# Expert, modulation and compression weights in slabs of 8 KB per partition, and two groups of thin products regrouped

## The chip, the cores and the metric
One core of a Trainium2 chip runs the whole program. The time is device microseconds of one execution from launch to end; lower is better. Times of the kernel before: 2248.72, 2251.83 and 2254.51 us, median 2251.83 us.

## What is computed
Three transformer blocks in a row on one sequence of 256 tokens with width 1024, all in float32, batch 1.

- Block 1: a normalized projection, two attention mixers (block attention with 8 heads, and an attention with compressed, selected and windowed keys, 8 heads), gates, an output projection. The compressed keys and values come from 15 windows of 32 tokens in two groups: `gelu(win @ w1) @ w2`, with w1 of 2048 x 256, once for keys and once for values.
- Block 2: two layers. Each is modulated by six vectors of 1024, `silu(c) @ ada_w + ada_b` with ada_w of 1024 x 6144 per layer (in the first layer, two of them for a second vector too). Layer 0 mixes by attention and a 31-tap convolution, layer 1 by a short convolution. Both end in 16 experts: each expert takes its 32 best tokens and computes `(silu(x @ gate) * (x @ up)) @ down`, three matrices of 1024 x 1024, that is 4 MB each. The experts of the two layers are 402 MB of weights, more than half of all that is read.
- Block 3: two layers with differential attention and gated linear attention, cross attention to a memory, and a feed-forward network with a 3-tap convolution.

## The kernel before
All loads of weights go through SyncE's queue (SP) in slabs of up to 1 MB, 128 partitions by 2048 floats. Buffers for them are the ring (`slab`, L320): four in block 1, seven in block 2.

*Dense weights* (`weights`, L383) come from one array that the host packs so that each slab is contiguous, 8 KB per partition. Each is split in pieces of 128 x 1024 into a high half `wh` (ACT, L376) and a rest `wl` (VectorE, L377), in two tiles with three buffers each. A dense product is three matmuls (L408 to L410): high by high, rest by high, high by rest. In `rows` the halves are the moving operand, in `columns` the stationary one. After each slab, `step` lets a generator (`fill`) put in some of the modulation's work.

*Modulation* (`Ada.steps`, L960): 12 chunks of 512 columns per layer, each in two slabs that take four rows of 2 KB per partition straight from the matrix (L975). In 6 of the 24 chunks VectorE multiplies and adds, in the other 18 PE does: the vector is the stationary operand with 32 columns, of which one or two are filled, and each of four row tiles has a column group of its own (L979), with 512 columns of output. The four groups are summed after an ACT copy (L1000), four transposes (L1002) and a VectorE sum (L1004).

*Compression* (`compress`, L724): windows `wn` are made from transposed keys and values (L738, L746). Each w1 comes in two slabs with eight rows of 1 KB per partition (L751). 16 products per matrix of 256 columns (L755) add up in one column group for keys and one for values. An element-wise chain (L758 to L766), two transposes (L769) and w2 (L775) follow. On POOL's queue the bias table of the attention is written to memory and read back meanwhile (`toeplitz`, L667 and L670); attention reads it first in `nsa(0)` (L605).

*Experts* (`moe`, L1320): a quarter of a matrix is a slab. `place` (L1338) puts slab after slab into a rotation of 21 places: seven buffers of the ring, seven of `more`, three pairs of split buffers (two DMAs of 512 KB), and four tiles that are free in this stage, one of them (`xv`) made of four quarters of 256 KB. A place is loaded again once PE has used it. The row tiles k and k + 1 stand in a partition as two rows of 4 KB. A slab is eight products of 256 columns on four column groups (L1359). Expert 15's down weights are taken by columns instead (`down`, L1487), in rows of 1 KB, so that output columns finish one after the other; then come the next layer's first steps.

The convolution of layer 0 (`gated`, L1115) writes its input to memory (L1128) and reads it back in four shifted copies (L1132), on SP's queue too.

The order of instructions on each engine is made by the compiler's scheduler from the program order, priorities and modelled durations; SP issues in that order and stops at each DMA whose buffer isn't free.

Of the kernel before, what the change touches and what calls it, by code (L numbers as in the profile page):

```python
# [87 lines left out]

def _pack_dense(inp):
    flat = np.empty(DENSE_SIZE, np.float32)  # L90
# [178 lines left out]
class Kern:  # L269
# [113 lines left out]
    def weights(self, key, g, chunks=None, gain=None):  # L383


        for at, k0, nk, width in (OFF[key][g] if chunks is None else [OFF[key][g][c] for c in chunks]):
# [286 lines left out]
def block1(k, ada):  # L673
# [4 lines left out]
    with ExitStack() as cx:  # L678
# [45 lines left out]
        def compress():  # L724
# [33 lines left out]
            h = ea.tile([64, 256], F32, name="cmp_x")  # L758
            nc.scalar.copy(h, hid[:64, :256])
            z = ea.tile([64, 256], F32, name="cmp_z")  # L760
# [7 lines left out]
            for f in range(2):  # L768
                nc.tensor.transpose(p[:, 64 * f:64 * f + 64], z[:, 128 * f:128 * f + 128], k.ident[:64, :64])  # L769
            ht = ea.tile([128, 2, 64], F32, name="cmp_ht")  # L770
            nc.scalar.activation(ht, p[:, :128].rearrange("p (f s) -> p f s", f=2), AF.Copy, scale=0.5)
# [171 lines left out]
class Ada:  # L943
# [16 lines left out]
    def steps(self, l, which, chunks=range(12)):  # L960
# [4 lines left out]
        for c in chunks:  # L965
# [7 lines left out]
            for h in range(2):  # L973
                w = k.slab(2048).rearrange("p (k f) -> p k f", f=512)
                nc.sync.dma_start(w, k.a["ada_w_2"][l, 512 * h:512 * h + 512, 512 * c:512 * c + 512].rearrange("(k p) f -> p k f", p=128))  # L975
                for kt in range(4):
                    if not vec:
                        with k.tc.issue_after(self.behind.ins) if self.behind is not None else ExitStack():
                            nc.tensor.matmul(acc[32 * kt:32 * kt + 32], self.st[:, 4 * h + kt], w[:, kt], start=h == 0, stop=h == 1,  # L979
                                             tile_position=(0, 32 * kt))  # L980
# [7 lines left out]
                if h == 1:  # L988
# [9 lines left out]
                    else:  # L998
                        ms = k.sm.tile([128, 512], F32, tag="sq", name="ada_ms", bufs=1)
                        nc.scalar.copy(ms, acc)  # L1000
# [1003 lines left out]
```

## Time and profile before

| | |
|---|---|
| profiled execution | 2254.34 us, span 2252.5 us |
| granted clock, mean | 0.888 |
| PE busy | 1853.4 us (82%), 14677 matmul instructions |
| VectorE busy | 1026.7 us (46%) |
| ACT busy | 723.6 us (32%) |
| DMA | 638.00 MB, mean 283 GB/s |
| block 1 | 0 to about 320 us |
| layer 0 up to the routing, experts | to about 540, to 994 us |
| short convolution, routing, experts | to about 1125, to 1577 us |
| block 3 | to the end |

PE's busy time counts pipelined matmuls, so a busy PE is not PE at its peak. A float32 product counts as two matmul instructions (x16 is eight products), a split one as one. The DMA share is the busy time of the 16 DMA engines and can pass 1, since a packet's record overlaps the next. A chain of waits is the work that ended last, followed back from the end: start, duration, engine or transfer, tile and line. A transfer in it lasts from issue to landing and so includes the time that it stands behind others.

### The profile page before, as it was taken

The page shows a single profiled execution, that of the slowest core. Times are in us where ns is not written, and L with a number is a line of the kernel's source. Part 1 is how long each engine was busy: PE and PEld are TensorE (multiplying, and loading weights), DVE is VectorE, ACT ScalarE, POOL GpSimd, SP SyncE. Part 2 cuts the span into 40 slices and gives each one's busy share as a digit, 9 for nine tenths or more (in the row PEclk, how much of TensorE's full clock was granted, in tenths as well). Part 3 has the DMA queues.
Part 4 walks back from the last instruction along what each step waited for, and adds up shares of the span by engine and source line. Part 5 has one row for each costly group of instructions (what it writes and reads, how often), then busy time and mean ns, then how long its engine had stood idle before and what let it go on. Part 6 is the DMA issues. An engine that isn't in the chain of part 4 may idle for free.

```text
span 2252.5 us, 35590 instructions
## 1 busy us (share of the span) xinstructions
PE 1853.4 (82%) x14677; PEld 1275.5 (57%) x14677; DVE 1026.7 (46%) x2282; ACT 723.6 (32%) x1360; POOL 53.0 (2%) x94
## 2 busy tenths in 40 slices
PE   7999998888766666679886666666998999999999
PEld 5777875455322222249642222222776998888997
DVE  5785675444100000048510000002876996678984
ACT  3444444342000000025300000001665665555663
POOL 1000010101000000000100000000100000000000
PEclk9999999998887777789897777777999999999999
DMA  9664588867999999997799999999632455344453
GB/s 256 238 211 167 204 299 285 295 227 259 408 408 408 408 408 405 408 396 303 258 404 408 408 408 408 406 408 393 199 133 79 165 187 178 123 138 160 171 178 121
DMA packets 176466, 638.00 MB, mean 283 GB/s; under 512 B 12158, under 2 KB 27390, under 8 KB 157872
## 3 DMA queue, kind: packets, MB, share of 16 engines
q1 hardware_dynamic: 173504, 627.03, 73.9%
q0 software_dynamic: 1360, 4.49, 1.1%
q10 hardware_dynamic: 1440, 4.21, 0.5%
q8 instruction: 115, 1.88, 0.3%
q14 instruction: 47, 0.39, 0.0%
HBM read 632.96 MB, written 2.72 MB: 282 GB/s over the span
## 4 chain that ended last, share of the span: by engine, by line
PE 51%; DMA 37%; DVE 6%; ACT 3%; issue 2%; SPq 0%; POOL 0%; ACTq 0%; DVEq 0%
DMA w<-in_moe_w_up 6%; DMA more<-in_moe_w_gate 4%; DMA wl<-in_moe_w_up 4%; PE up L410 4%; PE up L409 4%; PE up L408 4%; DMA more<-in_moe_w_up 3%; PE gu L1359 3%; DMA w<-in_moe_w_down 3%; DMA more<-in_moe_w_down 2%; PE down L408 2%; PE down L410 2%; PE down L409 2%; DMA wl<-in_moe_w_down 2%; DVE wl L377 2%
## 5 line engine op out<-in xcount | busy, mean ns | idle before, releaser
L377 DVE TENSOR_TENSOR wl<-w,wh 128x1024 fp32r<-128x1024 f32 (+5 forms) x316 | 377.3, 1198 | 172.5 <-ACT wh L376 165.7
L376 ACT CAST wh<-w 128x1024 fp32r<-128x1024 f32 (+5 forms) x316 | 320.7, 1021 | 285.4 <-PE down L409 63.4
L1458 ACT ACTIVATE hd<-gu 128x256 f32<-128x256 f32 x32 | 12.3, 384 | 746.5 <-PE gu L1359 746.5
L1459 DVE SCALAR_TENSOR_TENSOR hd<-hd,gu 128x256 f32<-128x256 f32 x32 | 13.5, 421 | 500.0 <-ACT hd L1458 500.0
L1359 PE MATMUL gu<-w,xst 128*32 128x256 f32 x1376 | 125.3, 496 | 74.2 <-DMA w<-in_moe_w_up 43.1
L409 PE MATMUL up<-ff_xh,wl 128*128 128x256 f32 x608 | 171.0, 283 | 2.7 <-DVE wl L377 2.7
L410 PE MATMUL up<-ff_xl,wh 128*128 128x256 f32 x608 | 170.1, 283 | 1.2 <-DVE ff_xl L377 1.2
L408 PE MATMUL up<-ff_xh,wh 128*128 128x256 f32 x608 | 168.5, 284 | 2.4 <-ACT ff_xh L376 2.4
L1359 PE MATMUL gu<-more,xst 128*32 128x256 f32 x1344 | 112.1, 466 | 56.3 <-DMA more<-in_moe_w_up 30.3
L1359 PEld LDWEIGHTS gu<-w,xst 128*32 128x32 f32 x1376 | 44.6, 132 | 150.2 <-DMA w<-in_moe_w_up 70.6
L409 PEld LDWEIGHTS up<-ff_xh,wl 128*128 128x128 f32 x608 | 116.2, 191 | 3.1 <-DVE wl L377 3.1
L1473 DVE SCALAR_TENSOR_TENSOR ysm<-dn,gcol,moe_mq 128x256 f32<-128x256 f32 x30 | 14.5, 484 | 226.7 <-PE dn L1359 226.7
L410 PEld LDWEIGHTS up<-ff_xl,wh 128*128 128x128 f32 x608 | 115.2, 190 | 1.5 <-DVE ff_xl L377 1.5
L408 PEld LDWEIGHTS up<-ff_xh,wh 128*128 128x128 f32 x608 | 114.4, 191 | 2.8 <-ACT ff_xh L376 2.8
L1359 PEld LDWEIGHTS gu<-more,xst 128*32 128x32 f32 x1344 | 44.7, 127 | 119.0 <-DMA more<-in_moe_w_up 53.4
L408 PE MATMUL down<-wh,ff_h 128*128 128x512 f32 x176 | 69.7, 396 | 0.0
L409 PE MATMUL down<-wh,ff_l 128*128 128x512 f32 x176 | 69.6, 396 | 0.0
L1359 PE MATMUL dn<-more,ht 128*32 128x256 f32 x672 | 56.3, 483 | 14.1 <-DMA more<-in_moe_w_down 9.6
L1359 PE MATMUL dn<-w,ht 128*32 128x256 f32 x672 | 56.9, 480 | 9.3 <-ACT ht L1465 5.2
L410 PE MATMUL down<-wl,ff_h 128*128 128x512 f32 x176 | 63.7, 395 | 0.0
L409 PE MATMUL w_in_b<-xh,wl 128*128 128x256 f32 x192 | 56.4, 295 | 2.8 <-DVE wl L377 2.8
L408 PE MATMUL w_in_b<-xh,wh 128*128 128x256 f32 x192 | 55.2, 296 | 2.0 <-ACT wh L376 2.0
(643 smaller groups left out, 4031.9 us busy)
## 6 DMA issues: line engine op xcount, KB each, us to landing
w<-in_wd SPq DMA_DIRECT2D x144, 1024.0 KB, 5.0
w<-in_ada_w SPq DMA_DIRECT2D x48, 1024.0 KB, 6.5
w<-in_moe_w_gate SPq DMA_DIRECT2D x48, 1024.0 KB, 14.6
more<-in_moe_w_up SPq DMA_DIRECT2D x48, 1024.0 KB, 18.5
w<-in_moe_w_down SPq DMA_DIRECT2D x46, 1024.0 KB, 18.0
more<-in_moe_w_down SPq DMA_DIRECT2D x46, 1024.0 KB, 18.6
w<-in_moe_w_up SPq DMA_DIRECT2D x38, 1024.0 KB, 15.6
more<-in_moe_w_gate SPq DMA_DIRECT2D x36, 1024.0 KB, 18.5
```

The lines of the kernel that those rows point to most:

```text
L376: self.nc.scalar.copy(hi, src)
L377: self.nc.vector.tensor_tensor(lo, src, hi.bitcast(F32), op=OP.subtract)
L408: mm(out, lh, rh, start=first, stop=False)
L409: mm(out, ll, rh, start=False, stop=False)
L410: mm(out, lh, rl, start=False, stop=last)
L1359: nc.tensor.matmul(out[32 * c:32 * c + 32], lhs(kt), w(1024 * kk + 256 * c, 256), start=kt == 0, stop=kt == 7, tile_position=(0, 32 * c))
L1458: nc.scalar.activation(hd, gu[:, 0:256], AF.Tanh, scale=0.5)
L1459: nc.vector.scalar_tensor_tensor(hd, hd, 1.0, gu[:, 0:256], op0=OP.add, op1=OP.mult)
L1473: nc.vector.scalar_tensor_tensor(y, dn[:, :256], gcol[:, e:e + 1], mq, op0=OP.mult, op1=OP.mult)
```

## The change
The host lays out the expert, modulation and first compression matrices anew, so that every slab is one contiguous megabyte with 8 KB per partition; expert 15's down weights in the order of its column quarters. The DMAs that load them take whole rows of 8 KB (only the place made of four quarters keeps four DMAs, with rows of 2 KB). To have an 8 KB place there too, `wh` and `wl` become the two halves of one tile `ws` with three buffers, for dense weights as for experts.

The compression product is split: each of keys and values is computed in two halves of 128 columns in two column groups, which makes four groups with 128 columns each. The chain behind it works on 128 x 128 instead of 64 x 256, with one transpose.

The modulation product keeps four column groups and uses them otherwise: row tiles kt and kt + 2 share one, and the 512 columns are split in two halves of 256. That makes 16 products of 256 columns per chunk instead of eight of 512, a copy of 256 columns, two transposes instead of four, and a sum over two groups, one sum per vector.

```diff
+def _lay_out(inp):
+    for n in ("moe_w_gate_2", "moe_w_up_2", "moe_w_down_2"):
+        w = inp[n]
+        s = w.reshape(2, 16, 4, 2, 128, 1024).transpose(0, 1, 2, 4, 3, 5).reshape(2, 16, 4, 128, 2048)
+        if n == "moe_w_down_2":
+            s = s.copy()
+            s[:, 15] = w[:, 15].reshape(2, 8, 128, 4, 256).transpose(0, 3, 2, 1, 4).reshape(2, 4, 128, 2048)
+        inp[n] = s
+    inp["ada_w_2"] = inp["ada_w_2"].reshape(2, 2, 4, 128, 12, 512).transpose(0, 4, 1, 3, 2, 5).reshape(2, 12, 2, 128, 2048)
+    for n in ("cmp_w1_k", "cmp_w1_v"):
+        inp[n] = inp[n].reshape(1, 2, 8, 128, 256).transpose(0, 1, 3, 2, 4).reshape(1, 2, 128, 2048)
...
-                wh, wl = (self.sp.tile([128, 1024], F32R, tag=z, name=z)[:, :m * width].rearrange("p (k c) -> p k c", c=width)
-                          for z in ("wh", "wl"))
+                ws = self.sp.tile([128, 2048], F32R, tag="ws", name="ws")
+                wh, wl = (ws[:, z:z + m * width].rearrange("p (k c) -> p k c", c=width) for z in (0, 1024))
...
-                    nc.sync.dma_start(w.rearrange("p (l f) -> p l f", f=256),
-                                      a[nm][1024 * half:1024 * half + 1024].rearrange("(l p) f -> p l f", p=128))
+                    nc.sync.dma_start(w, a[nm][half])
                     for l in range(8):
                         lp = 8 * half + l
-                        nc.tensor.matmul(hid[32 * i:32 * i + 32, :256], wn[:, i, lp].rearrange("p g c -> p (g c)"),
-                                         w[:, 256 * l:256 * l + 256], start=lp == 0, stop=lp == 15,
-                                         tile_position=(0, 32 * i))
+                        for f in range(2):
+                            b = 32 * (2 * i + f)
+                            nc.tensor.matmul(hid[b:b + 32, :128], wn[:, i, lp].rearrange("p g c -> p (g c)"),
+                                             w[:, 256 * l + 128 * f:256 * l + 128 * f + 128], start=lp == 0, stop=lp == 15,
+                                             tile_position=(0, b))
...
-                nc.sync.dma_start(w, k.a["ada_w_2"][l, 512 * h:512 * h + 512, 512 * c:512 * c + 512].rearrange("(k p) f -> p k f", p=128))
+                nc.sync.dma_start(w.rearrange("p k f -> p (k f)"), k.a["ada_w_2"][l, c, h])
...
-                            nc.tensor.matmul(acc[32 * kt:32 * kt + 32], self.st[:, 4 * h + kt], w[:, kt], start=h == 0, stop=h == 1,
-                                             tile_position=(0, 32 * kt))
+                            for z in range(2):
+                                q0 = 32 * (2 * (kt % 2) + z)
+                                nc.tensor.matmul(acc[q0:q0 + 32, :256], self.st[:, 4 * h + kt], w[:, kt, 256 * z:256 * z + 256],
+                                                 start=h == 0 and kt < 2, stop=h == 1 and kt > 1, tile_position=(0, q0))
...
-        sp = lambda: [k.sp.tile([128, 1024], F32, tag=z, name=z) for z in ("wh", "wl")]
+        sp = lambda: [k.sp.tile([128, 2048], F32, tag="ws", name="ws")]
...
-            w = place(a[name][l, e, 256 * h:256 * h + 256].rearrange("(k p) f -> p k f", p=128), (own, xp) if e == 15 else ())
+            w = place(a[name][l, e, h], (own, xp) if e == 15 else ())
...
-            w = place(a["moe_w_down_2"][l, 15, :, 256 * h:256 * h + 256].rearrange("(k p) f -> p k f", p=128), (xw, xv, own, xp))
+            w = place(a["moe_w_down_2"][l, 15, h], (xw, xv, own, xp))
```

## Rows read from the trace of the kernel before

**Rows 1.** Busy tenths and rate of the DMA engines in 40 slices (page, part 2).
```profile
DMA  9664588867999999997799999999632455344453
GB/s 256 238 211 167 204 299 285 295 227 259 408 408 408 408 408 405 408 396 303 258 404 408 408 408 408 406 408 393 199 133 79 165 187 178 123 138 160 171 178 121
```
**Rows 2.** Stretches: length, busy time of PE, PEld, DVE, ACT, POOL, clock, DMA.
```profile
540.00:975.00 435.00, 294.22 (x3276) 120.30 (x3276) 35.05 (x75) 17.38 (x40) 0.00 (x0) 0.79 1.02 402
...
1140.00:1560.00 420.00, 272.75 (x3052) 106.72 (x3052) 27.79 (x64) 12.15 (x31) 0.00 (x0) 0.77 1.03 406
...
996.00:1010.00 14.00, 13.07 (x108) 11.51 (x106) 12.24 (x29) 10.12 (x25) 0.27 (x6) 1.00 1.02 419
...
975.00:987.00 12.00, 7.02 (x66) 2.20 (x66) 2.11 (x10) 0.76 (x2) 0.00 (x0) 0.83 1.05 360
```
**Rows 3.** Chain of waits in and at the end of the expert stages.
```profile
785.19 1.97 PE gu L1359 x16
...
787.25 18.37 DMA w<-in_moe_w_down
...
975.26 12.80 DMA w<-in_moe_w_down
...
988.20 1.93 PE last L1493 x16
...
1560.37 13.32 DMA w<-in_wd
```
**Rows 4.** DMA packets by size, 700 to 800 us, then 996 to 1010 us.
```profile
DMA packets 11234, 40.78 MB, mean 408 GB/s; under 512 B 785, under 2 KB 785, under 8 KB 11227
...
DMA packets 805, 5.87 MB, mean 419 GB/s; under 512 B 90, under 2 KB 90, under 8 KB 90
```
**Rows 5.** Chain of waits at the compression.
```profile
38.18 16.82 DMA w<-in_cmp_w_v
55.04 3.64 PE cmp_h L755 x16
```
**Rows 6.** Timeline at the compression, of PE, DVE and SP's queue.
```profile
43.15 6.65 PE L755 MATMUL cmp_h<-w,wn 128*32 128x256 f32 x32
...
43.92 2.18 DVE L746 TENSOR_TENSOR wn<-kd,t 64x256 f32<-64x256 f32 x4 [0.97 <-ACT kd L740]
...
46.82 0.34 SPq L390 DMA_DIRECT2D w<-in_wd  x1
```
**Rows 7.** DMA queues, 42 to 51 us: packets, MB, share of 16 engines.
```profile
q0 software_dynamic: 364, 1.29, 69.4%
q1 hardware_dynamic: 560, 0.57, 35.0%
```
**Rows 8.** Chain of waits: transposes of a modulation chunk, its products, an expert slab.
```profile
380.82 0.44 PE ada_t L1002 x4
...
385.71 1.90 PE ada L979 x16
...
543.65 1.00 PE gu L1359 x16
```
**Rows 9.** Chain of waits: first scores with the bias table, copies of the convolution.
```profile
103.50 0.42 PE sc L595 x2
...
354.67 7.20 DMA evd<-ev_w
...
363.22 9.90 DMA ev_w<-evd
...
468.54 2.95 DMA ev_w<-evd
```
**Rows 10.** Split weights: costliest group (page, part 5), and waits of 1580 to 2252 us.
```profile
L377 DVE TENSOR_TENSOR wl<-w,wh 128x1024 fp32r<-128x1024 f32 (+5 forms) x316 | 377.3, 1198 | 172.5 <-ACT wh L376 165.7
...
ACT wh L376 <- PE down L409: 63.4, 39, 2.2
...
PE up L409 <- DVE wl L377: 2.7, 2, 1.8
```

More of the change, by code (lines that the diff above doesn't have):

```diff
@@ L86 @@
 OFF, DENSE_SIZE = _offsets()
+def _lay_out(inp):
[9 more added lines that the diff above has]
+        inp[n] = inp[n].reshape(1, 2, 8, 128, 256).transpose(0, 1, 3, 2, 4).reshape(1, 2, 128, 2048)
 def _pack_dense(inp):
+    _lay_out(inp)
     flat = np.empty(DENSE_SIZE, np.float32)
@@ L750, in compress @@
                     w = k.slab(2048)
-                    nc.sync.dma_start(w.rearrange("p (l f) -> p l f", f=256),
-                                      a[nm][1024 * half:1024 * half + 1024].rearrange("(l p) f -> p l f", p=128))
+                    nc.sync.dma_start(w, a[nm][half])
                     for l in range(8):
                         lp = 8 * half + l
-                        nc.tensor.matmul(hid[32 * i:32 * i + 32, :256], wn[:, i, lp].rearrange("p g c -> p (g c)"),
-                                         w[:, 256 * l:256 * l + 256], start=lp == 0, stop=lp == 15,
-                                         tile_position=(0, 32 * i))
-            h = ea.tile([64, 256], F32, name="cmp_x")
-            nc.scalar.copy(h, hid[:64, :256])
-            z = ea.tile([64, 256], F32, name="cmp_z")
+                        for f in range(2):
[3 more added lines that the diff above has]
+                                             tile_position=(0, b))
+            h = ea.tile([128, 128], F32, name="cmp_x")
+            nc.scalar.copy(h, hid[:, :128])
+            z = ea.tile([128, 128], F32, name="cmp_z")
             c0 = math.sqrt(2.0 / math.pi)
@@ L767, in compress @@
             p = k.gen("cmp_t")
-            for f in range(2):
-                nc.tensor.transpose(p[:, 64 * f:64 * f + 64], z[:, 128 * f:128 * f + 128], k.ident[:64, :64])
+            nc.tensor.transpose(p[:, :128], z, k.ident)
             ht = ea.tile([128, 2, 64], F32, name="cmp_ht")
-            nc.scalar.activation(ht, p[:, :128].rearrange("p (f s) -> p f s", f=2), AF.Copy, scale=0.5)
+            nc.scalar.activation(ht.rearrange("p f (i s) -> p f i s", i=2), p[:, :128].rearrange("p (i f s) -> p f i s", i=2, f=2),
+                                 AF.Copy, scale=0.5)
             p = k.gen("cmp_o")
@@ L998, in steps @@
                     else:
-                        ms = k.sm.tile([128, 512], F32, tag="sq", name="ada_ms", bufs=1)
-                        nc.scalar.copy(ms, acc)
-                        for i in range(4):
+                        ms = k.sm.tile([128, 512], F32, tag="sq", name="ada_ms", bufs=1)[:, :256]
+                        nc.scalar.copy(ms, acc[:, :256])
+                        for i in range(2):
                             nc.tensor.transpose(p[:, 128 * i:128 * i + 128], ms[:, 128 * i:128 * i + 128], k.ident)
-                        r = k.small(8, "hss8")[:, :4 * nv].rearrange("p (i v) -> p i v", v=nv)
-                        nc.vector.tensor_reduce(r, p.rearrange("p (i c s) -> p i s c", i=4, s=32)[:, :, 0:nv], axis=AX.X, op=OP.add)
-                        nc.vector.tensor_tensor(out, r, bias, op=OP.add)
+                        r = k.small(8, "hss8")[:, :4 * nv].rearrange("p (v z i) -> p v z i", v=nv, z=2)
+                        for v in range(nv):
+                            nc.vector.tensor_reduce(r[:, v], p[:, :256].rearrange("p (i q z s) -> p z i s q", i=2, q=2, s=32)[:, :, :, v],
+                                                    axis=AX.X, op=OP.add)
+                        nc.vector.tensor_tensor(out, r.rearrange("p v z i -> p (z i) v"), bias, op=OP.add)
             yield 1
@@ L1344, in place @@
             turn[0] += 1
-            size, f = 2048 // len(ts), src.shape[-1]
+            size = 2048 // len(ts)
             for j, w in enumerate(ts):
-                at, m = size * j, min(f, size)
-                w = w.rearrange("p (k f) -> p k f", f=m)
                 with tc.issue_after(hold.ins) if hold is not None else ExitStack():
-                    nc.sync.dma_start(w, src[:, at // f:at // f + size // m, at % f:at % f + m])
+                    nc.sync.dma_start(w, src[:, size * j:size * j + size])
             return lambda at, n: ts[at // size][:, at % size:at % size + n]
         def part(out, name, e, h, lhs):
-            w = place(a[name][l, e, 256 * h:256 * h + 256].rearrange("(k p) f -> p k f", p=128), (own, xp) if e == 15 else ())
+            w = place(a[name][l, e, h], (own, xp) if e == 15 else ())
             for kk in range(2):
```

## The prediction
> **What bounds the kernel now.** First the busy line of the DMA engines in 40 slices [rows 1]: two long plateaus, slices 11 to 18 and 21 to 28, stand at 9 with about 408 GB/s. Those are the two expert stages. Cut by time [rows 2] they are 540 to 975 us and 1140 to 1560 us: the DMA share is 1.02 and 1.03, the rate 402 and 406 GB/s, while PE is busy 294 of 435 and 273 of 420 us, DVE and ACT hardly at all. In the chain of waits of such a stage [rows 3] one weight slab follows the other, each issued when PE has released a buffer and landing some 18 us later, with two microseconds of PE between some of them. Many slabs are in flight and the engines never pause, so it is a slab's moving time that sets the stage, not its latency and not PE. The stage ends the same way: the last down slab lands at 975.26 + 12.80 = 988.06 us and PE's last products start at once; in the second stage the chain passes through a dense load issued at 1560.37, which is queued behind the last down slabs. Outside these stages the chain runs mostly through PE's products, except for two places where it goes through transfers: the compression weights, 38 to 58 us [rows 5], and the shifted copies of the convolution [rows 9].
>
> **Expert slabs, rows of 4 KB to 8 KB.** On the plateau, 700 to 800 us, 11,227 of 11,234 packets are under 8 KB, and the mean is 408 GB/s [rows 4]. What 8 KB rows do is shown by the dense weights, which are laid out so already: from 996 to 1010 us only such rows were moved (and the small packets that signal completion), 5.87 MB in 14 us, 419 GB/s, with the engines as full (share 1.02) and with PE and DVE busier than in the expert stages [rows 2, 4]. A slab of 1.0486 MB therefore takes 2.570 us at 408 and 2.503 us at 419, 0.067 us less. The plateaus hold 435 x 402 = 174.9 MB and 420 x 406 = 170.5 MB, together 329 slabs. One place in 21 of the rotation (the four quarters of "xl") keeps rows of 2 KB, so 314 slabs gain: 21 us. All of it is on the path, since the transfers set the end and PE has a third of the time free. Bounds: 0, if 408 is a ceiling of something other than the row; 40 us above, if the pause between packets went altogether. I take 21, from the stretch that is the operation itself.
>
> The Trainium skill (DMA: Bandwidth & Descriptors, Why small descriptors are slow) gives each packet a fixed overhead of about 3 cycles beside one cycle per 32 bytes. By that 4 KB would be 131 cycles and 8 KB 259, a gain of 1.1%, as an estimate from that page 9 us instead of 21. The two windows differ by 2.7%, and the measurement decides.
>
> **Down weights of expert 15.** These eight slabs were cut in columns, so their rows are 1 KB. The window 975 to 987 us, mostly theirs, shows 360 GB/s [rows 2], 2.91 us a slab against 2.50: 0.41 x 8 = 3.3 us, at the very end of both stages, where nothing hides it (bounds 0 and 4.2, the latter if the part at 4 KB is taken out of the window).
>
> **Compression weights and products.** Four slabs in rows of 1 KB. The last is issued at 38.18 us and lands 16.82 us later [rows 5], because the bias table is being read on POOL's queue: from 42 to 51 us q0 moved 364 packets with 1.29 MB and q1 560 packets with only 0.57 MB [rows 7]. So the queues share by packets rather than bytes, and a larger packet brings q1 more per turn. A q0 packet takes 0.694 x 16 x 9 / 364 = 0.275 us; an 8 KB packet 1.008 x 16 x 14 / 712 = 0.317 us (the packets of [rows 4] without the small ones). Eight rows per engine, one for one with q0, are 8 x 0.59 = 4.7 us, so the slab lands near 43 us. The Trainium skill (same page, Queues, rings and completion order) says that an engine round-robins between queue rows at packet granularity; the counts above agree.
>
> The products: eight of 256 columns in one column group take 3.64 us a slab [rows 5]. Split in two halves on two groups, eight pairs of 128 columns take half, 1.8 us; that groups run side by side is seen in the expert products, where eight of 256 columns on four groups take 1.00 us [rows 8]. Then: k's first slab 43.15 to 45.0; v's waits for its windows, DVE until 43.92 + 2.18 = 46.10 [rows 6]; three slabs from there end at 51.5 instead of 58.68: 7.2 us. Next on the path is the slab of row group 5, issued on SP at 46.82 us when the first compression slab is released [rows 6]; that release comes at 45.0 and the load no longer stands behind a late slab, so it moves along. The two modulation slabs and the rest of the group behind it on SP are issued at releases by the same products and shift as well. What is delayed is the bias table: the last compression slab, row group 5's and two modulation slabs take 2.5 + 1.3 + 5 = 9 us of the engines before it. It is read first after the scores at 103.50 us [rows 9], some 40 us later. Bounds: 1.8 us (the slab still lands at 55.0 and only its products halve) and 7.2 us. I take 6. The element-wise chain behind it (64x256 tiles to 128x128, one transpose instead of two) lies beside row group 5's products: 0.
>
> **Modulation.** 18 of 24 chunks go through PE. Eight products of 512 columns take 1.90 us; sixteen of 256 on the same four groups are twice the expert pattern, 2 x 1.00 us [rows 8]: +0.10 x 18 = +1.8 us. Two transposes of four go, 0.44 to 0.22 us: -0.22 x 18 = -4.0 us. Net -2.2 us of PE, which is on the path in most of these stretches; bounds -4 and +2 (if the doubled weight loads show). The loads from 2 KB to 8 KB rows are paced by buffers, not by the engines, whose share is between 4 and 9 tenths there [rows 1]; but the round trips of the convolution queue behind them, six transfers of 3 to 10 us in the chain, the first two and the last shown [rows 9], 39 us in all. 5% of it is 2 us, bounds 0 and 4. ACT's copy and DVE's sums lie beside PE's dense products. I take 3 of the 4.2 us, since the pieces overlap.
>
> **One tile for both halves of a split.** Some 54 pairs of half-slab DMAs become whole ones: SP issues less, the bytes are the same, 0. For the dense products a buffer comes free when the later half has been read, one product later than now for the other half. There are three buffers, and it is ACT that waits for PE there (63.4 us in 39 waits in one group) and PE hardly for DVE (2.7 us in two) [rows 10]: two further pieces' products hide it. 0; if that cover were gone, see the third rival.
>
> **Sum.** 21 + 3.3 + 6 + 3 = 33 us. The profiled execution took 2254.34 us (span 2252.5), 2.5 us over the median of the runs and inside their spread. 2254.34 - 33 = 2221; on the median, 2251.83 - 33 = **2219 us**.
>
> **Rivals.**
> 1. *408 GB/s is a ceiling of the source or of the ports, and long rows don't lift it over hundreds of microseconds.* For it: the 419 come from a stretch of 14 us. Against: the engines were equally full, and it is no peak between pauses. Then the 21 us go: 3.3 + 6 + 3 = 12, 2240 us. The Trainium skill (same page, Specifications) puts the HBM limit of a core at about 358 GB/s; the plateau at 408 already passes it, so here that is not the bound.
> 2. *The compression gain ends in another wait*: row group 5's slab waits among the bias reads as the compression slab does now. For it: q0 holds two thirds of the engines there [rows 7]. Against: the row's packets are larger. 24.3 + 3 + 0 = 27, 2225 us, inside the range.
> 3. *The joined split tile costs PE.* If the first product of a piece must wait for both halves, it waits for DVE's subtraction too, 1.198 us on average over 316 pieces [rows 10]. For it: PE uses the high half first. Against: PE's waits for DVE are nearly nil, so pieces are ready early. It decides from 33 / 1.2 = 28 exposed pieces on; with 70 of the 316 it is 84 - 33 = 51 us slower, 2303 us.
>
> **Numbers.** Forecast 0.70, rival 1 0.13, rival 2 0.12, rival 3 0.05. A measurement of this kernel tells 0.3% (7 us) from no change. All but rival 3 are faster by more than that, and a few cases of rival 3 only eat up the gain: faster 0.92, same 0.04, slower 0.04. Range 2203 to 2237: the lower end is a gain of 29 (half way to the bound) + 4 + 7 + 8 = 48, the upper end one of 15 (10 + 3 + 2 + 0); rivals 1 and 3, 0.18, are left out.
>
> **What would show it.** Plateaus at 417 to 422 GB/s and both expert stages some 12 us shorter; the last down slabs at the same rate as the others; the last compression product ending near 51 instead of 58.7 us; two transposes per chunk. It is wrong if the plateau stays at 408, or if PE's waits for split weights grow from a few to tens of microseconds.

## The result and the profile after

| | before | after |
|---|---|---|
| median of 4 runs each, side by side | 2250.27 us | 2224.32 us |
| lowest to highest | 2246.73 to 2254.51 | 2220.56 to 2226.26 |
| ratio, 95% interval | | 0.9883 [0.9863, 0.9903] |
| profiled execution, its span | 2254.34, 2252.5 us | 2224.66, 2222.9 us |

The change is 26 us faster on the medians and 29.6 us on the two profiled spans; 33 were predicted (2219 us, range 2203 to 2237).

The busy line of the DMA engines after, in 40 slices, answers to [rows 1].

```profile
DMA  8654578766999999997699999999632455344553
GB/s 252 249 218 162 213 296 298 291 233 226 418 418 418 418 418 418 418 411 299 259 414 418 418 418 418 419 419 397 181 124 95 162 181 179 125 150 145 180 180 123
```

Both plateaus stand at 418 GB/s where they stood at 408. Cut by time (columns as in [rows 2]): the two expert stages, then the last down slabs of either stage.

```profile
538.00:965.00 427.00, 293.90 (x3280) 122.64 (x3283) 34.86 (x75) 17.38 (x40) 0.00 (x0) 0.77 1.00 411
...
1126.00:1536.00 410.00, 270.81 (x3072) 109.12 (x3060) 27.79 (x64) 12.15 (x31) 0.00 (x0) 0.77 1.01 418
...
961.00:973.00 12.00, 6.65 (x66) 2.39 (x66) 2.05 (x10) 0.62 (x2) 0.00 (x0) 0.78 1.02 419
...
1528.00:1540.00 12.00, 7.99 (x67) 2.77 (x66) 1.33 (x3) 0.76 (x2) 0.00 (x0) 0.69 1.02 422
```

PE's busy time in a stage is what it was (293.90 against 294.22 us); only the transfers are shorter, and the last down slabs, at 360 GB/s before, keep the plateau's rate. On the plateau (here 640 to 740 us) the packets under 8 KB are now the small ones and those of the place made of four quarters, against nearly all in [rows 4]:

```profile
DMA packets 6601, 41.82 MB, mean 418 GB/s; under 512 B 733, under 2 KB 733, under 8 KB 1757
```

The chain of waits still runs from slab to slab, up to the dense load behind the last one, as in [rows 3]: the stages have the same bound as before.

```profile
606.20 19.93 DMA more<-in_moe_w_gate
626.20 19.86 DMA ws<-in_moe_w_down
646.12 12.46 DMA w<-in_moe_w_up
...
949.09 16.79 DMA xv<-in_moe_w_up
...
965.94 17.09 DMA w<-in_wd
```

Two products cut the span in three where this change is to be told from the rest: the first `gather` (the experts begin) and the first `mkv` (block 3, just behind the second expert stage). The view by tile gives their first and last start; before, then after.

```profile
L1437 PE MATMUL gather<-oh,xr x64: 387/393/504, 539.2 to 1124.9; 128*128 128x512 f32 x64
L408 PE MATMUL mkv<-wh,yh x32: 390/393/486, 1607.1 to 1646.4; 128*128 128x512 f32 x32
```
```profile
L1456 PE MATMUL gather<-oh,xr x64: 387/395/504, 537.1 to 1110.5; 128*128 128x512 f32 x64
L424 PE MATMUL mkv<-ws,yh x32: 390/393/497, 1581.7 to 1622.6; 128*128 128x512 f32 x32
```

| stretch, us | before | after | predicted | measured |
|---|---|---|---|---|
| start to first gather (compression, modulation) | 539.2 | 537.1 | -9 | -2.1 |
| first gather to first mkv (both expert stages) | 1067.9 | 1044.6 | -24.3 | -23.3 |
| first mkv to the end (nothing of the change but the joined split tile) | 645.4 | 641.2 | 0 | -4.2 |

Each kernel was profiled once, and the first and the third row can't carry what they seem to say. The changed kernel and three of those below (expert rows of 4 KB, expert rows of 2 KB, expert 15's down rows of 1 KB) have the same order of instructions on every engine up to the first gather, and differ there at most in the rows of the first expert slabs, which land from about 440 us on; yet the first gather starts at 537.1, 538.4, 528.3 and 535.3 us. The earliest, with 2 KB rows:

```profile
L1461 PE MATMUL gather<-oh,xr x64: 387/394/505, 528.3 to 1137.1; 128*128 128x512 f32 x64
```

So the 2.1 us of the front stand in a scatter of 10 us; what the front gave is told better by the times (only the expert layout, below). The 4.2 us at the end came where none were forecast, in a stretch where all kernels with this code differ by as much (last section).

The expert stages can be cut more sharply: from the first expert product, `gu`, to the landing of the stage's last down slab. The first products of both stages before, then after:

```profile
543.58 1.07 PE L1359 MATMUL gu<-w,xst 128*32 128x256 f32 x16
1119.13 1.07 PE L1359 MATMUL gu<-w,xst 128*32 128x256 f32 x16
541.40 1.07 PE L1378 MATMUL gu<-w,xst 128*32 128x256 f32 x16
1104.72 1.07 PE L1378 MATMUL gu<-w,xst 128*32 128x256 f32 x16
```

The last down slab of the first stage, before and after, with the us from its issue (981.93 before, 965.27 after) to its landing; in the second stage the last one lands at 1569.14 and 1542.63:

```profile
more<-in_moe_w_down SPq DMA_DIRECT2D x1, 1024.0 KB, 12.1
...
more<-in_moe_w_down SPq DMA_DIRECT2D x1, 1024.0 KB, 14.3
```

The stages so cut are 450.4 and 450.0 us before, 438.2 and 437.9 after: 900.4 and 876.1 together, 24.3 us less. In six other kernels below whose expert rows are as in the changed one the sum lies between 875.9 and 877.4, so this length repeats within 1.5 us, and it is used below as *the length of both stages*. The expert term came out.

At the compression, the chain after (answers to [rows 5]), then the timeline of VectorE and PE (answers to [rows 6]), and the issue of the last slab with the us to its landing:

```profile
46.21 1.97 PE cmp_h L772 x32
48.19 6.06 DMA w<-in_wd
...
70.90 4.98 DMA w<-in_ada_w
```
```profile
47.99 2.13 DVE L762 TENSOR_TENSOR wn<-kd,t 64x256 f32<-64x256 f32 x4
...
50.18 6.24 PE L772 MATMUL cmp_h<-w,wn 128*32 128x128 f32 x96 [2.03 <-DVE wn L762]
```
```profile
w<-in_cmp_w_v SPq DMA_DIRECT2D x1, 1024.0 KB, 13.4
```

The products do take half, 1.97 us a slab instead of 3.64. But values' windows are made at 47.99, four microseconds later than the 43.92 of before, and the last slab, issued at 38.50, lands at 51.9 where 43 was predicted. The last product ends at 56.4 us; 51.5 was predicted, 58.7 is before. A part of that is the clock: these 96 products took 6.24 us at a mean granted clock of 0.72, and 4.69 us at 1.00 in the kernel with expert rows of 4 KB, whose instructions here are the same (last section).

### The profile page after: what moved, and what is told of

It is laid out like the page before. It is cut to its first block, busy times and chain, and to the rows that moved or that the text cites. A ratio compares the mean times of both kernels' runs of the same rounds, so it can differ in the third digit from the quotient of the medians.

```text
span 2222.9 us, 36003 instructions
## 1 busy us (share of the span) xinstructions
PE 1832.6 (82%) x14992; PEld 1279.2 (58%) x14992; DVE 1028.9 (46%) x2284; ACT 721.3 (32%) x1360; POOL 51.9 (2%) x94
## 4 chain that ended last, share of the span: by engine, by line
PE 47%; DMA 41%; DVE 7%; ACT 3%; issue 2%; SPq 0%; POOL 0%; ACTq 0%; DVEq 0%
DMA more<-in_moe_w_gate 5%; DMA w<-in_moe_w_gate 4%; DMA more<-in_moe_w_up 4%; DMA ws<-in_moe_w_down 4%; DMA ws<-in_moe_w_gate 4%; DMA more<-in_moe_w_down 4%; DMA ws<-in_moe_w_up 4%; PE up L426 3%; PE up L425 3%; PE up L424 3%; DMA w<-in_moe_w_down 3%; DMA w<-in_moe_w_up 3%; DMA w<-in_wd 2%; DVE ws L393 2%; PE down L426 2%; PE down L424 2%
## 5 line engine op out<-in xcount | busy, mean ns | idle before, releaser
L393 DVE TENSOR_TENSOR ws<-w,ws 128x1024 fp32r<-128x1024 f32 (+5 forms) x316 | 377.3, 1197 | 179.1 <-ACT ws L392 174.8
L392 ACT CAST ws<-w 128x1024 fp32r<-128x1024 f32 (+5 forms) x316 | 321.1, 1021 | 268.7 <-PE down L426 63.8
L425 PE MATMUL up<-ff_xh,ws 128*128 128x256 f32 x608 | 169.5, 281 | 4.3 <-DVE ws L393 4.3
L426 PE MATMUL up<-ff_xl,ws 128*128 128x256 f32 x608 | 168.4, 280 | 1.8 <-DVE ff_xl L393 1.8
L424 PE MATMUL up<-ff_xh,ws 128*128 128x256 f32 x608 | 167.8, 281 | 2.4 <-ACT ff_xh L392 2.4
L1378 PE MATMUL gu<-more,xst 128*32 128x256 f32 x1344 | 109.0, 456 | 51.5 <-DMA more<-in_moe_w_up 29.0
L425 PEld LDWEIGHTS up<-ff_xh,ws 128*128 128x128 f32 x608 | 115.0, 189 | 5.0 <-DVE ws L393 5.0
L426 PEld LDWEIGHTS up<-ff_xl,ws 128*128 128x128 f32 x608 | 114.5, 189 | 2.1 <-DVE ff_xl L393 2.1
L424 PEld LDWEIGHTS up<-ff_xh,ws 128*128 128x128 f32 x608 | 113.8, 189 | 2.9 <-ACT ff_xh L392 2.8
L1378 PE MATMUL gu<-ws,xst 128*32 128x256 f32 x608 | 51.9, 469 | 24.3 <-DMA ws<-in_moe_w_up 13.8
L424 PE MATMUL down<-ws,ff_h 128*128 128x512 f32 x176 | 69.7, 396 | 0.0
L425 PE MATMUL down<-ws,ff_l 128*128 128x512 f32 x176 | 69.5, 395 | 0.0
L426 PE MATMUL down<-ws,ff_h 128*128 128x512 f32 x176 | 63.9, 396 | 0.0
L425 PE MATMUL w_in_b<-xh,ws 128*128 128x256 f32 x192 | 56.9, 299 | 1.8 <-DVE ws L393 1.8
```

Of the source, the lines that this page charges most:

```text
L392: self.nc.scalar.copy(hi, src)
L393: self.nc.vector.tensor_tensor(lo, src, hi.bitcast(F32), op=OP.subtract)
L424: mm(out, lh, rh, start=first, stop=False)
L425: mm(out, ll, rh, start=False, stop=False)
L426: mm(out, lh, rl, start=False, stop=last)
L1378: nc.tensor.matmul(out[32 * c:32 * c + 32], lhs(kt), w(1024 * kk + 256 * c, 256), start=kt == 0, stop=kt == 7, tile_position=(0, 32 * c))
```

## Experiments

In the first four, T1 says that a packet costs a fixed time beside its bytes, so that the row's length alone gives the gain; T2 that the joined split tile and the new order of instructions do.

**Expert rows back to 4 KB, all else changed.** The host cuts a slab in two blocks of 4 KB per partition (expert 15's down slabs in eight of 1 KB):

```diff
+        s = s.reshape(2, 16, 4, 128, 2, 1024).transpose(0, 1, 2, 4, 3, 5).reshape(2, 16, 4, 128 * 2048)
...
-                    nc.sync.dma_start(w, src[:, size * j:size * j + size])
+                    nc.sync.dma_start(w.rearrange("p (k f) -> p k f", f=m), src[:, at // f:at // f + size // m, at % f:at % f + m])
```


> The changed kernel with the expert weights in rows of 4 KB again (expert 15's down weights in rows of 1 KB); all else as changed. Theory 1, a packet costs a fixed time beside its bytes: a slab took 2.570 us at 408 GB/s and 2.509 us at 418, 0.0615 us for 8 packets per engine, 7.7 ns each. Then 313 slabs take 19 us more and expert 15's eight slabs 3.4 us, 23 us over the changed kernel: 2247 us, plateaus at 408 GB/s. Theory 2, the gain comes from the joined split tile and from another order of instructions: within 8 us of the changed kernel, below 2233 us.

Measured: 2247.72 us, ratio to before 0.9983 [0.9973, 0.9993]. The whole gain but 3 us is gone. First gather to first mkv is 1067.6 us (before 1067.9) and the length of both stages 901.0 (before 900.4), so in that stretch it is the rows and nothing else. T1.

**Expert rows of 2 KB** (the same with `4, 512`; expert 15 stays at 8 KB).

> The changed kernel with the expert weights in rows of 2 KB (expert 15's down weights stay at 8 KB). Theory 1: 24 packets more per engine and slab than at 8 KB, 0.185 us, a slab 2.69 us, plateaus at 389 GB/s; 313 slabs make 58 us more than the changed kernel, 2282 us. Rival, rows of 4 KB lose by something that belongs to 4 KB (the step between a partition's two rows) and not by the number of packets: 2 KB rows at about 408 GB/s, near 2247 us.

Measured: 2292.68 us, ratio 1.0193 [1.0173, 1.0212]. The same stretch of the plateau, with rows of 4 KB, then of 2 KB:

```profile
700.00:800.00 100.00, 62.10 (x684) 23.94 (x680) 5.88 (x14) 3.02 (x8) 0.00 (x0) 0.77 1.03 408
```
```profile
700.00:800.00 100.00, 64.93 (x646) 24.42 (x646) 5.18 (x13) 2.65 (x7) 0.00 (x0) 0.67 1.05 387
```

The engines are full in all three (share 1.01 to 1.05); the rate goes 387, 408, 418 (the changed kernel's plateau as shown above; 419 in just these 100 us). A slab of 1.0486 MB takes 2.710, 2.570 and 2.509 us. An engine moves a sixteenth, in 32, 16 or 8 packets: 0.140 us for 16 packets more and 0.061 for 8 are 8.7 and 7.6 ns a packet (8.4 instead of 7.6 with 419). T1, a little over the 7.7 ns expected; the time is 10 us over T1's 2282, and the length of both stages, 944.2 us, is 68 over the changed kernel's where 58 were expected.

**Only the expert layout, on the kernel before** (compression, modulation and split tiles as before, so the three split places still take two DMAs of 4 KB rows).

```diff
-            w = place(a[name][l, e, 256 * h:256 * h + 256].rearrange("(k p) f -> p k f", p=128), (own, xp) if e == 15 else ())
+            w = place(a[name][l, e, h], (own, xp) if e == 15 else ())
```


> The kernel before with only the expert weights laid out in 8 KB rows; the places made of two split tiles keep two DMAs with rows of 4 KB. Theory 1: 266 of 329 slabs gain 0.0615 us, 16 us, and expert 15's eight slabs 3.4 us: 20 us less than before, 2230 us. Theory 2: less than half of the 26 us, above 2238 us.

Measured: 2229.27 us, ratio 0.9907 [0.989, 0.9924]: 21.5 of the 26 us from this part alone. T1. This kernel also says what the rest of the change is worth: the two ratios differ by 0.0024, 5 us, and 3.8 of them lie in the expert stages (length 879.9 us against 876.1, by the places with 4 KB rows). Some 2 us are left for compression, modulation and the joined tile together, with an interval of about 6 us to either side; 9 were forecast.

**Split tiles apart again.**

```diff
-                ws = self.sp.tile([128, 2048], F32R, tag="ws", name="ws")
-                wh, wl = (ws[:, z:z + m * width].rearrange("p (k c) -> p k c", c=width) for z in (0, 1024))
+                wh, wl = (self.sp.tile([128, 1024], F32R, tag=z, name=z)[:, :m * width].rearrange("p (k c) -> p k c", c=width)
+                          for z in ("wh", "wl"))
```


> The changed kernel with the halves of a split in two tiles again, and two DMAs for these places (rows of 4 KB). Theory 1: 47 slabs at 4 KB are 2.9 us more than the changed kernel, 2227 us; the dense products of the last block are as long as in the changed kernel. Theory 2: the joined tile brought the 4 to 5 us by which the last block is shorter than the expert stages explain, so 2232 us, and those microseconds are gone in the last block's trace.

Measured: 2229.53 us, ratio 0.991 [0.9893, 0.9928], between the two; the intervals of this kernel and the changed one overlap. The length of both stages is 879.3 us, 3.2 longer where T1 has 2.9, by the three places with 4 KB rows. Block 3, where a joined tile could cost PE, is 645.2 us with tiles apart and 641.2 joined, which is what T2 expected. But it is not the tile: of the ten other kernels with the joined tile seven have a block 3 of 644.4 to 646.1 us and three one of 640.4 to 641.3, and the two other kernels with tiles apart 645.4 and 643.6. What parts them is the pace of the last section; at the same pace joined and apart are alike within 2 us. So the joined tile shows neither a gain nor a cost beyond that (third rival). In the changed kernel PE's wait for the rest of a split, with its count and longest:

```profile
PE up L425 <- DVE ws L393: 4.3, 3, 1.8
```

**Compression products in two groups again**, slabs as changed.

```diff
-                        for f in range(2):
-                            b = 32 * (2 * i + f)
-                            nc.tensor.matmul(hid[b:b + 32, :128], ...
+                        nc.tensor.matmul(hid[32 * i:32 * i + 32, :256], ...
```


> The changed kernel with the compression products as they were: 16 products of 256 columns per matrix in one column group for keys and one for values, weights still in rows of 8 KB. In the changed kernel the last product ends at 56.4 us and the last slab lands at 51.9 us. Theory A (the products' halving is worth what it says, and was hidden behind later windows and the late slab): a slab's products take 3.64 us instead of 1.9, two of the four slabs are behind the last wait, so the last product ends about 3.5 us later, near 60 us, and the time is 2 to 4 us longer, 2227. Rival (the products wait for slabs anyway): the last product moves by one slab's 1.8 us at most, 2224 to 2226.

Measured: 2225.57 us, ratio 0.9884 [0.9864, 0.9905]. The last product ends at 59.4, 3 us later as A has it; the time doesn't follow as far as can be told (the interval leaves room for A's 2 to 4 us). Row group 5's slab is issued at 50.20, two microseconds later, and lands after 4.5, at 54.7 us, half a microsecond later. Both theories took the end of the products for the path.

**Compression rows of 1 KB again**, products as changed.

```diff
-                    nc.sync.dma_start(w, a[nm][half])
+                    nc.sync.dma_start(w.rearrange("p (l f) -> p l f", f=256),
+                                      a[nm][1024 * half:1024 * half + 1024].rearrange("(l p) f -> p l f", p=128))
```


> The changed kernel with only the compression weights back in rows of 1 KB; the four-group products stay. Theory A (a queue's turn is a packet, so a larger row gives this queue more per turn): the last of the four slabs lands again some 16 to 17 us after its issue instead of 13.4, near 55 us, and the last product ends 2 to 4 us later than the 56.4 of the changed kernel. Rival (what holds the slab is the bias table on the other queue whatever the rows): landing near 52 and last product near 56 as in the changed kernel, no change of time (2224).

Measured: 2224.97 us, ratio 0.988 [0.9863, 0.9896]. The last slab lands at 53.8 us (51.9 with 8 KB), the last product ends at 56.5: it waits for the windows in both, and the time is the rival's. The row's length does matter on the queues. From 42 to 51 us (packets, MB, share of 16 engines; POOL's queue is q0), rows of 1 KB, then of 8 KB:

```profile
q0 software_dynamic: 356, 1.26, 68.7%
q1 hardware_dynamic: 608, 0.62, 35.7%
```
```profile
q1 hardware_dynamic: 168, 1.16, 51.4%
q0 software_dynamic: 303, 1.08, 50.6%
```

Against [rows 7] and the run with 1 KB, SP's queue moves almost twice the bytes. But it gets one packet for two of q0, not one for one. And from 38.5 to 42 us, behind the slab's issue, it gets nearly nothing (some 2 us of that are a slab's start even without the bias reads: 4.7 us to landing, below, against 2.5 of moving):

```profile
q0 software_dynamic: 182, 0.66, 101.8%
q1 hardware_dynamic: 3, 0.01, 1.2%
```

The Trainium skill (DMA: Bandwidth & Descriptors, Queues, rings and completion order) says that an engine goes round its queue rows packet by packet; if its packets are those of the profile, 168 to 303 here, and 608 to 356 with 1 KB, are not a turn each; nor are the 560 to 364 of [rows 7], which the prediction took to agree. No run here shows what else decides.

**Windows ahead of row group 3.** In program order the transposes and window sums stand first; nothing else is changed.

```diff
+        windows()
         qb = raw()
         row_group(3, qb)
         compress()
```


> The changed kernel with the making of the compression windows (transposes of keys and values, copies, window sums) put ahead of row group 3 in program order, nothing else. In the changed kernel keys' windows are ready at 46.2 and values' at 50.1 us, because the scheduler set a head-norm reduction between them. Theory A (this order took the rest of the predicted gain): both windows are ready by 45 us, products end near 52 to 53, 3 to 4 us earlier, and the time is near 2221. Rival (the last slab's landing at 52 us decides): the products end 1.5 to 2 us after the landing, near 54, a gain of 2 us at most (2222 to 2224); if row group 3 is delayed by the windows instead, nothing is gained or some is lost.

Measured: 2220.71 us, ratio 0.9866 [0.9848, 0.9884]. The products end at 53.3 us as A expects. But the first scores with the bias table start at 101.3 us, against 101.2 in the changed kernel. The chain of this kernel shows what comes between:

```profile
44.00 1.90 PE cmp_h L775 x32
45.91 8.44 DMA w<-in_wd
...
70.93 5.14 DMA w<-in_ada_w
```

Row group 5's slab is issued 2.3 us earlier (45.91, not 48.19) and takes 8.44 instead of 6.06 us: it lands at 54.35 and 54.25. The modulation slab behind it starts at 70.93 and 70.90. The time gained at the products is waited out at the next slab. That the first scores start no earlier doesn't prove it by itself: in the kernels with the changed kernel's order of instructions they start anywhere from 101.2 to 104.6 us. The difference of 3.6 us in the medians (the intervals overlap) isn't explained by these lines. The two profiles differ by 3.8 us between those scores and the first gather (533.3 us), and by 4.1 from there to the first mkv (1040.5 us), of which 2.9 lie between the two expert stages and 1.6 at the hand-over to block 3. The kernels with the changed kernel's order of instructions differ among themselves by 9 us between first scores and first gather, and by 3 between the stages.

**Bias reads held until the compression is over**, on top of the windows first. A one-column POOL copy into the table makes its reads wait for the hidden values.

```diff
             nc.scalar.copy(h, hid[:, :128])
+            nc.gpsimd.tensor_copy(bias[:, 0, 0:1], h[:, 0:1])
+            read_bias()
```


> The kernel with the windows put first, and the four reads of the bias table on POOL's queue held back until the compression's hidden values have been copied. With the windows first the last compression slab was issued at 37.9 us and landed 13.4 us later while the bias reads held about half of the engines, and the last product ended at 53.3 us. Theory A (the bias reads hold the slab, whatever its rows): without them the slab lands 3 to 5 us after its issue, near 42, v's windows (46.8 us) decide instead, the last product ends near 49, and the slab of row group 5 comes earlier too: 3 to 5 us less than with the windows first alone (2220.7), some 2216 to 2218. Rival B (the transfers come back as soon as they are let go: the reads then stand beside row group 5's slab and the modulation slabs, which are late instead): the last product ends near 49 all the same, but the time is within 2 us of 2220.7 or above it.

Measured: 2220.08 us, ratio 0.9864 [0.9841, 0.9887]. From 36 to 80 us, issues by tile (count, KB each, median us to landing):

```profile
w<-in_wd SPq DMA_DIRECT2D x3, 1024.0 KB, 13.9
bias<-tdram POOLq DMA_DIRECT2D x4, 512.0 KB, 16.1
...
w<-in_cmp_w_v SPq DMA_DIRECT2D x1, 1024.0 KB, 4.7
```

The slab lands in 4.7 us instead of 13.4, so it was the bias reads that held it, and the prediction's 43 us is reached (37.95 + 4.7 = 42.7). The last product ends at 51.9, where both theories had 49: the windows were ready only at 47.2. But now the dense slabs of 1 MB take 13.9 us (6.6 in the same stretch with the windows first alone), PE waits for their splits, and the chain goes through a modulation slab:

```profile
PE w_in_b L424 <- ACT ws L392: 5.7, 1, 5.7
PE w_in_a L424 <- ACT ws L392: 3.9, 1, 3.9
```
```profile
51.91 9.33 DMA w<-in_wd
63.68 14.11 DMA w<-in_ada_w
```

The first scores start at 104.7, and the time is that of the windows first alone. Rival B: the 2.1 MB that POOL reads delayed the compression slab where they stood, and delay the slabs behind it where they stand now.

**Modulation products as before**, slabs of 8 KB rows.

```diff
-                                nc.tensor.matmul(acc[q0:q0 + 32, :256], self.st[:, 4 * h + kt], w[:, kt, 256 * z:256 * z + 256], ...
+                            nc.tensor.matmul(acc[32 * kt:32 * kt + 32], self.st[:, 4 * h + kt], w[:, kt], ...
```


> The changed kernel with the modulation products as they were (eight of 512 columns per chunk, four transposes, four-group sum); weights still in rows of 8 KB. In the changed kernel a chunk's products take the same 1.9 us and two transposes instead of four are left. Theory A (two transposes less are 0.22 us of PE in 18 chunks, on the path in most): 2 to 4 us longer, 2227. Rival (these stretches are held by transfers and by the products' order, not by the transposes): 2222 to 2226, no difference that can be told.

Measured: 2223.16 us, ratio 0.9865 [0.9845, 0.9885]: no difference that can be told, the rival.

**Modulation rows of 2 KB again.**

```diff
-                nc.sync.dma_start(w.rearrange("p k f -> p (k f)"), k.a["ada_w_2"][l, c, h])
+                nc.sync.dma_start(w, k.a["ada_w_2"][l, 512 * h:512 * h + 512, 512 * c:512 * c + 512].rearrange("(k p) f -> p k f", p=128))
```


> The changed kernel with only the modulation weights back in four rows of 2 KB per partition. By the prediction's term (transfers around the convolution's round trips 5% shorter, 2 us, bounds 0 and 4) the time is 2225 to 2228. By the packet times measured in the expert stages (a slab takes 0.20 us longer in rows of 2 KB than in rows of 8 KB), 48 slabs are 9.6 us of transfers, but they are loaded where the engines have pauses, so nearly all is hidden: 2224 to 2225, no difference that can be told.

Measured: 2227.51 us, ratio 0.9889 [0.9872, 0.9906]. Its median lies 3 us above the changed kernel's, the ratios only 0.0006 apart: inconclusive, and no sign of more than the 3 us of the prediction's term. The first two round trips of the convolution, which that term was about, take 28.7 us with rows of 2 KB, 29.1 with 8 KB and 29.5 before: the rows don't show in them.

**Expert 15's down rows of 1 KB again** (`place(..., 8)` for these slabs alone).

> The changed kernel with only expert 15's down weights back in rows of 1 KB, eight slabs in all at the ends of the two expert stages. By the prediction's term, 0.41 us a slab at 360 GB/s: 3.3 us longer, 2227 to 2228. By the time per packet from the rows of 2 and 4 KB (7.7 to 8.4 ns) a slab in 1 KB rows takes 0.43 to 0.47 us longer: 3.4 to 3.8 us, about the same. Rival (the dense loads queued behind them have slack, or PE's last products decide): under 1 us, 2224 to 2225.

Measured: 2225.38 us, ratio 0.9881 [0.9864, 0.9898]: not told apart on the medians. In the profile the last down slabs of the two stages (stretches as shown above for the changed kernel) move at

```profile
961.00:973.00 12.00, 7.45 (x74) 2.75 (x70) 1.99 (x10) 0.76 (x2) 0.00 (x0) 0.64 1.01 339
```
```profile
1528.00:1540.00 12.00, 8.23 (x71) 2.94 (x66) 1.45 (x4) 0.76 (x2) 0.00 (x0) 0.64 1.02 318
```

instead of 419 and 422 GB/s. They land 3.0 us apart instead of 2.5, which is 8.9 ns for each of the 56 packets more per engine and slab, and the length of both stages is 880.0 us, 3.9 more than in the changed kernel and clear of the 1.5 us by which it scatters. So the term of 3.3 us is there, with about 3.9; that it reaches the end isn't shown by the times.

**Only rows of 8 KB in the experts**, on top of the windows first: the place of four quarters is left out after its first use.

```diff
-            while places[turn[0] % len(places)] in free:
+            while places[turn[0] % len(places)] in free or turn[0] >= len(places) and places[turn[0] % len(places)] is xv:
```


> The kernel with the windows put first, and the place made of four quarters (rows of 2 KB) left out of the experts' rotation after its first use in each stage, so that some 15 slabs that had rows of 2 KB get rows of 8 KB and 20 places are left. Theory A (a packet costs a fixed time, 0.20 us more for a slab in rows of 2 KB than in rows of 8 KB, and transfers set both stages): the plateau rises from 418 to about 419.5 GB/s, the stages shorten by 3 us together, and the time is 2217 to 2218 (2220.7 with the windows first alone). Rival (one buffer less in the rotation makes the transfers wait for PE, or the gap between the stages is longer): the plateau stays at or under 418 with pauses, and the time is 2221 or more.

Measured: 2220.61 us, ratio 0.9854 [0.9827, 0.988]. The plateau rises by about 1 GB/s, as A has it; this kernel in two stretches:

```profile
640.00:740.00 100.00, 63.30 (x698) 24.26 (x694) 5.39 (x13) 2.27 (x6) 0.00 (x0) 0.78 1.01 419
1200.00:1500.00 300.00, 197.55 (x2124) 75.09 (x2116) 17.49 (x41) 7.56 (x20) 0.00 (x0) 0.75 1.01 419
```

But the length of both stages is 876.4 us in both kernels. The first is 1.6 us shorter (437.1 against 438.7). The second is 439.3 against 437.8, because a load of 962 KB for block 3 (`t`, on ACT's queue) is issued earlier, at 1522.36 instead of 1534.05 us, and moves among the last down slabs: two of these land 3.4 and 4.0 us after the one before instead of 2.5. Without these 2.4 us the two stages would be 2.5 us shorter, near A's 3. The stretch between the stages is longer too, 125.9 against 122.2 us, as the rival has it, within what other kernels show (122.0 to 127.2). So A is right on the transfers, and the time is that of the windows first. Neither this kernel nor the one with the windows first nor the one with the bias reads held can be told from the changed kernel (their intervals overlap its 0.9883 [0.9863, 0.9903]).

## Why the prediction was right, and where not

- *What bounds the kernel, and the 21 + 3.3 us of the experts: right.* 418 GB/s was in the forecast band of 417 to 422. Both stages together are 24.3 us shorter, as summed, and rows of 4 KB give all of it back. That it fits to the decimal is luck: expert 15's down slabs brought about 3.9 us instead of 3.3, the others about 20.4 instead of 21. One reading was wrong without harm: the slab that lands at 988.06 us is the second of the four last down slabs; the last lands at 994.01. (The place called "xl" is `xv`.) The first rival (408 is a ceiling) is refuted. Eight-KB dense rows in a 14 us stretch were a fair sample of 400 us, since they had the same full engines.
- *By the Trainium skill's overhead* (DMA: Bandwidth & Descriptors, Why small descriptors are slow), 1.1% was the estimate for 4 to 8 KB. The runs show 2.4% (408 to 418) and 5.4% from 2 to 4 KB: the fixed time of a packet is more than twice what the page's 3 cycles give.
- *Compression, 6 us: the step that failed.* Two things in it were wrong. "Eight rows per engine, one for one with q0" put the slab's landing at 43 us; the queue got one packet for two and nearly none in the first 3.5 us, and it was 51.9. And "that release comes at 45.0 ... so it moves along" took row group 5's slab to follow the products. It doesn't: issued anywhere from 45.4 to 50.2 us, it lands between 53.8 and 55.2 in all eleven kernels with new compression code or rows, as long as the bias reads stand beside it (with the reads held at 49.9). Before it was issued at 46.82 and took 9.5 us, to 56.4. Some 2 us of the 6 are left at that landing; whether they reach the end isn't shown, since the first scores (103.4 before, 101.2 after) scatter from 101.2 to 104.6 with one and the same order of instructions. That this slab waits among the bias reads is the second rival, whose 2225 us is within a microsecond of the median. The range held the forecast and this rival alike, so that the time fell into it says nothing for the compression term. The windows' later place (47.99) and the clock hid this in the changed kernel; putting the windows first moved the products, not the next landing.
- *Modulation, 3 us: too much.* Half the transposes went as forecast, and 16 products of 256 columns take what eight of 512 took, 1.91 against the 1.90 us of [rows 8]; the changed kernel's chain, then its transposes by line:

```profile
380.17 1.91 PE ada L998 x32
```
```profile
L1021 PE MATMUL ada_t<-t,ada_ms x36: 270/273/331, 75.6 to 437.9; 128*128 128x128 f32 x36
```

  Undoing the products changes nothing that can be told; undoing the rows is inconclusive (above). So no run shows the 3 us. The round trips of the convolution behind them are 7.95 and 8.45 us for the first (7.20 and 9.90 in [rows 9]).
- *Joined split tile, 0: right.* PE's wait for the rest grew from 2.7 us in two waits [rows 10] to 4.3 in three, not to tens.
- *The sum.* 33 us were forecast and 26 measured on the medians: 24.3 in the expert stages, where they were forecast, and about 2 for all the rest instead of 9. (The range's lower end takes 29 us for half way from 21 to 40; that is 30.5, and the end moves by 1.5 us.) The further 4.2 us of the profiled pair lie in block 3 and are no part of the change's mechanism as far as shown.

## What to carry to other kernels

Where the engines are full for hundreds of microseconds, take the rate of the longest-row transfer in the same trace as the price of longer rows, and believe it; the number of packets is then a cost like bytes. Where a stage is a weave of queues, a product that ends earlier is worth only what the next slab's landing allows: look for that landing before counting. And where the scheduler orders instructions anew with each edit, compare stretches between two fixed events, not only whole times, and look first how much such a stretch differs between profiles of kernels that are the same in it: here 1.5 us for the stages that transfers bound, 10 us for the front.

## What the hardware showed unexpectedly

- A packet costs 7.6 to 8.9 ns beside its bytes on full engines, from four row lengths (1 KB in expert 15's down slabs, 2, 4 and 8 KB on the plateaus).
- The same products run at two paces at a full granted clock. In the second feed-forward of block 3, 50 us from each kernel's steady part with PE always busy; the changed kernel, then the one with compression rows of 1 KB:

```profile
2093.00:2143.00 50.00, 50.00 (x444) 50.00 (x443) 47.02 (x84) 35.58 (x55) 0.00 (x0) 1.00 0.56 199
```
```profile
2098.00:2148.00 50.00, 50.00 (x426) 50.00 (x426) 45.13 (x82) 33.31 (x54) 0.00 (x0) 1.00 0.55 190
```

  444 products against 426, 4% apart. Of the fourteen profiled kernels four are at 443 to 444, before and nine others at 426 to 427, none between. Block 3 takes 640.4 to 641.3 us in the four and 643.6 to 646.1 in the others, so this is most of the 4.2 us. The order of instructions doesn't decide it: on every engine that of the changed kernel is the same throughout block 3 in five others, of which one (expert rows of 2 KB) is at 443 and four at 426 to 427. Nor does the chip alone, since two chips each ran kernels of both paces. What does stays open: each kernel was profiled once.
- The granted clock can fall behind a short pause of PE, and need not. In the changed kernel PE stood idle for 2.03 us before the last 96 compression products, and while they ran the mean granted clock was 0.72, between its two levels (1.2 and 2.4 GHz). The kernel with expert rows of 4 KB has the same products behind the same 2.03 us, at 1.00; with the bias reads held they followed a pause of 1.06 us, at 1.00 as well. The changed kernel, then the one with expert rows of 4 KB:

```profile
50.20:56.30 6.10, 6.10 (x96) 5.55 (x96) 2.78 (x14) 1.22 (x2) 0.00 (x0) 0.72 0.83 241
```
```profile
49.10:53.70 4.60, 4.60 (x96) 4.35 (x96) 1.70 (x11) 0.00 (x0) 0.00 (x0) 1.00 1.03 291
```
